# A feed-forward block with seven-product tiles: the token sums are spread over three tiles instead of four

## The chip, the cores and the metric

One Trainium2 chip, one core. The metric is the device time of one execution in microseconds; the median of several runs counts. One execution was profiled.

## The reference

One step of a small hybrid decoder: 512 prompt tokens and 64 sample tokens (8 sequences of 8), width 1024, two layers, all in float32. Each layer has two half-weighted SwiGLU feed-forward blocks around a mixer:

```python
def swiglu(x, wi, wo):
    gate, up = jnp.split(x @ wi, 2, axis=-1)
    return (jax.nn.silu(gate) * up) @ wo
...
h = h + 0.5 * swiglu(rms_norm(h, w['norm_w'][i, 0]), w['ffn1_wi'][i], w['ffn1_wo'][i])
# ... mixer: RWKV-7 in layer 0, dilated window attention in layer 1
h = h + 0.5 * swiglu(rms_norm(h, w['norm_w'][i, 2]), w['ffn2_wi'][i], w['ffn2_wo'][i])
```

The hidden width is 2816. The attention adds a bias that comes from a small table of 32 distance buckets for each head and dilation.

## The kernel before, in words

**Layout.** Activations lie transposed: 128 channels on partitions, 576 tokens along the free axis, in two halves of 288 (h0, h1). The 1024 channels are 8 groups of 128. Each float32 operand is split in a high part (a cast on ScalarE, ACT) and a low part (a subtraction on VectorE, DVE, or on GpSimd, POOL), and a product takes three TensorE passes: high x high, high x low, low x high. Each stretch of weights (128 x 512, 256 KB, tile `wr` or `sr`) is loaded by the queue of SyncE (SP) into one of three buffers, split to `wh`, `wl` (or `sh`, `sl`), and its raw buffer is free for the next load when its last reader is done.

**Two of the four feed-forward blocks are "fast"** (`ffn(..., fast=...)`): the first of layer 0, from 20 us on, and the second of layer 1, from 2450 us on. The hidden width is cut into 22 tiles of 128 columns.

- Tiles 0 to 4 (`pair`) are standard: gate and up, each in two token halves, in four PSUM banks `ps_e`. DVE scales the gate banks by the row norm (L365), ACT applies SiLU, POOL multiplies by the norm again (L368), DVE multiplies the up banks in (L371) and the result is split (L155). Tile 4 goes through its inputs in the outer loop, so it needs all four banks at once.
- Tiles 5 to 21 (`pair7`) take the input and weights as 2 x 2 blocks (channel halves by token halves; weight quarters 11, 21, 22, 12) and make seven block products instead of eight (L390), from sums of weight quarters (`seven`: s1 = 21 + 22, s2 = s1 - 11, s4 = 12 - s2 on DVE at L337, in PSUM; `ss` = 11 - 21 on POOL at L346) and sums of token quarters. Products are issued as 0 to 6 on three banks; bank A is used by products 0, 2, 4 and 6, and is copied or added between them (L396, L402, L407).
- Behind tiles 8, 16 and 21 comes an output part (`wo_part`, L422) on TensorE.

**The token sums** (`forms`) need the normalised input, which the standard tiles do not. For each k of 0 to 3 a step makes from the two channel groups k and k + 4 the products a and b (L292), then c = [a1 - a0, b1 - a1] (halves on DVE L294 and POOL L295) and d = [b1 - c0, b0 - d0] (DVE L296, POOL L297), and splits c and d into `TH`, `TL`. A last step, `quarters`, splits the token quarters a0, b0, b1 into the tiles `x`. The list of these five steps runs one behind each of the tiles 0 to 4 (L437).

**What sets the order.** The program is written tile after tile; a scheduler places each instruction into its engine's queue, and each engine works through its queue in order, waiting on semaphores. So a DVE instruction that waits holds up all behind it.

**The bias tables** are made in the first feed-forward block behind the mixer of layer 0 (1150 to 1240 us): a one-hot matrix `oh` (33 x 1160) is loaded and multiplied by the bias in three pieces (L1288), three times.

## Time and profile before

| | us |
|---|---|
| median of 3 runs (2924.57 to 2925.61) | 2925.57 |
| the profiled execution | 2930.93 |
| its span | 2928.8 |
| TensorE (PE) busy | 2786.2 (95%) |
| DVE busy | 1386.5 (47%) |
| ACT busy | 1198.0 (41%) |
| POOL busy | 1454.0 (50%) |
| mean granted TensorE clock | 0.975 of full speed |

TensorE is busy nearly all the time; the question for any change is which of its few waits it moves. Busy times of the other engines are averages over stages with different limits: in the first 120 us of a fast block DVE, ACT and POOL have the token sums to make beside the weights.

### The profile page before, as it was taken

Reading aid. Unit: us, or ns where it says so; the run is one execution under the profiler, and the core shown is the slowest. Engines: PE = TensorE matmul, PEld = TensorE weight load, DVE = VectorE, ACT = ScalarE, POOL = GpSimd, SP = SyncE. Lnnn points to the kernel's source line nnn. Section 1 sums busy time; section 2 is a strip of 40 time slices with the busy share of each in tenths; the row PEclk is TensorE's granted clock in tenths of the full one; section 3 lists DMA queues with packets and bytes.
Section 4 is the critical chain, followed back from the end, with each engine's and each line's share of the span. In section 5 each row is a group of like instructions: output and inputs, shape, how many; then the busy total and the mean of one; then the engine's idle time right before and its main releaser. Section 6 shows DMA issues by size and latency. Waiting matters only on the chain.

```text
span 2928.8 us, 56127 instructions
## 1 busy us (share of the span) xinstructions
PE 2786.2 (95%) x22360; PEld 2604.7 (89%) x22360; DVE 1386.5 (47%) x2940; ACT 1198.0 (41%) x2296; POOL 1454.0 (50%) x1196
## 2 busy tenths in 40 slices
PE   7899988988999999999999999999999999899997
PEld 7899987977776778999999999999888879899997
DVE  5533338467667654211226321122577775524345
ACT  4434345443333224222335422233456655435354
POOL 6756557553323335444544454454544326757553
PEclk9999998999989899999999999999999999999999
DMA  3233233222113112222233322223433443233223
GB/s 120 81 91 91 87 111 127 70 57 64 44 43 79 40 50 73 85 82 85 83 91 103 96 82 84 83 86 108 131 84 98 132 147 105 80 88 94 87 78 103
DMA packets 177082, 257.81 MB, mean 88 GB/s; under 512 B 46889, under 2 KB 68849, under 8 KB 176820
## 3 DMA queue, kind: packets, MB, share of 16 engines
q1 hardware_dynamic: 148736, 223.56, 25.4%
q10 hardware_dynamic: 28084, 30.66, 3.8%
q8 instruction: 176, 2.88, 0.4%
q14 instruction: 86, 0.70, 0.1%
HBM read 234.31 MB, written 19.85 MB: 87 GB/s over the span
## 4 chain that ended last, share of the span: by engine, by line
PE 71%; DVE 9%; issue 3%; ACT 2%; POOL 2%; DMA 1%; ACTq 0%; DVEq 0%; SPq 0%; POOLq 0%
PE ps_e L196 39%; PE ps_d L517 10%; PE ps_e L390 6%; PE ps_i L517 2%; PE ps_q L517 2%; PE ps_s L517 2%; PE ps_w L517 2%; PE ps_x L517 1%; PE ps_o L517 1%; PE ps_d L390 1%; DVE AR L583 1%; PE ps_pt L526 1%; DVE S L1307 1%; PE ps_d L196 1%; PE ps_y L517 1%
## 5 line engine op out<-in xcount | busy, mean ns | idle before, releaser
L170 POOL TENSOR_TENSOR wl<-wr,wh 128x512 fp32r<-128x512 f32 (+2 forms) x613 | 777.2, 1272 | 975.8 <-ACT wh L169 926.7
L196 PE MATMUL ps_e<-x,wh 128*128 128x288 f32 x3968 | 797.3, 296 | 13.0 <-ACT x L261 7.9
L169 ACT CAST wh<-wr 128x512 fp32r<-128x512 f32 (+2 forms) x613 | 362.2, 594 | 931.7 <-PE ps_e L196 723.8
L196 PEld LDWEIGHTS ps_e<-x,wh 128*128 128x128 f32 x3968 | 639.6, 189 | 18.7 <-ACT x L261 7.9
L196 PE MATMUL ps_e<-hv,wh 128*128 128x288 f32 x2944 | 587.8, 295 | 3.2 <-POOL hv L155 1.9
L196 PE MATMUL ps_e<-x,wl 128*128 128x288 f32 x1984 | 586.5, 296 | 1.4 <-POOL wl L170 1.4
L196 PEld LDWEIGHTS ps_e<-hv,wh 128*128 128x128 f32 x2944 | 472.6, 188 | 4.1 <-POOL hv L155 2.4
L196 PE MATMUL ps_e<-hv,wl 128*128 128x288 f32 x1472 | 434.2, 295 | 1.2 <-POOL wl L170 1.2
L517 PE MATMUL ps_d<-x,wh 128*128 128x288 f32 x1664 | 370.9, 310 | 7.0 <-DVE q L1370 3.3
L196 PEld LDWEIGHTS ps_e<-x,wl 128*128 128x128 f32 x1984 | 373.8, 189 | 2.0 <-POOL wl L170 1.9
L517 PEld LDWEIGHTS ps_d<-x,wh 128*128 128x128 f32 x1664 | 276.1, 192 | 27.5 <-issue 9.3
L196 PEld LDWEIGHTS ps_e<-hv,wl 128*128 128x128 f32 x1472 | 276.8, 188 | 1.5 <-POOL wl L170 1.4
L517 PE MATMUL ps_d<-x,wl 128*128 128x288 f32 x832 | 251.2, 302 | 0.1
L422 DVE SCALAR_TENSOR_TENSOR h<-ps_e,h 128x288 f32<-128x288 f32 x160 | 73.0, 456 | 366.1 <-PE ps_e L196 365.9
L371 DVE TENSOR_TENSOR u<-ps_e,t 128x288 f32<-128x288 f32 x108 | 48.3, 457 | 251.2 <-POOL t L368 142.9
L517 PEld LDWEIGHTS ps_d<-x,wl 128*128 128x128 f32 x832 | 159.9, 192 | 2.2 <-issue 0.5
L365 DVE TENSOR_TENSOR t<-ps_e,rs 128x288 f32<-128x288 f32 x108 | 48.9, 456 | 177.5 <-PE ps_e L196 177.5
L390 PE MATMUL ps_e<-TH,wh 128*128 128x288 f32 x408 | 120.9, 296 | 4.1 <-DVE ev L407 4.0
L390 PE MATMUL ps_e<-TH,wl 128*128 128x288 f32 x408 | 120.3, 295 | 0.0
L390 PE MATMUL ps_e<-TL,wh 128*128 128x288 f32 x408 | 120.2, 295 | 0.0
L1378 POOL TENSOR_TENSOR QS<-q,QS 64x512 fp32r<-64x512 f32 x48 | 63.4, 1321 | 69.2 <-ACT QS L1376 66.6
L332 POOL TENSOR_TENSOR wl<-wr,wh 128x512 fp32r<-128x512 f32 x68 | 88.9, 1310 | 8.7 <-ACT wh L331 5.6
(394 smaller groups left out, 5168.0 us busy)
## 6 DMA issues: line engine op xcount, KB each, us to landing
wr<-in_f1wi SPq DMA_DIRECT2D x142, 256.0 KB
wr<-in_f2wi SPq DMA_DIRECT2D x142, 256.0 KB
wr<-in_f1wo SPq DMA_DIRECT2D x72, 256.0 KB
wr<-in_f2wo SPq DMA_DIRECT2D x72, 256.0 KB
wr<-in_wrkv SPq DMA_DIRECT2D x48, 256.0 KB
wr<-in_wq SPq DMA_DIRECT2D x48, 256.0 KB
sr<-in_f1wi SPq DMA_DIRECT2D x34, 256.0 KB
sr<-in_f2wi SPq DMA_DIRECT2D x34, 256.0 KB
```

The costliest lines, as they stand in the source:

```text
L169: nc.scalar.copy(H, raw)
L170: nc.gpsimd.tensor_tensor(L, raw, H.bitcast(F32), op=ALU.subtract)
L196: nc.tensor.matmul(ps[0:nw], a, b[:, sl], start=k + m == 0, stop=3 * k + m == n - 1)
L332: eng.tensor_tensor(L, a, H.bitcast(F32), op=ALU.subtract)
L365: nc.vector.tensor_tensor(t1[:, sl], ps, rs[:, sl], op=ALU.mult)
L371: nc.vector.tensor_tensor(u[:, sl], ps, t1[:, sl], op=ALU.mult)
L390: nc.tensor.matmul(ps, a, b, start=first and k + m == 0, stop=k == DT // 2 - 1 and m == 2, skip_group_check=True)
L422: nc.vector.scalar_tensor_tensor(h[:, sl], ps, 0.5, h[:, sl], op0=ALU.mult, op1=ALU.add)
L517: self.nc.tensor.matmul(out, lhsT, rhs, **kw)
L526: self.nc.tensor.transpose(out, in_, ident)
L583: nc.vector.scalar_tensor_tensor(m, self.xx[k], self.vec(name, k), self.xn[k], op0=ALU.mult, op1=ALU.add)
L1378: nc.gpsimd.tensor_tensor(qp[H2[1 - par], par], q[o, 0:TP], qp[o, par].bitcast(F32), op=ALU.subtract)
```

## The change

The five steps are spread by a table: step 0 behind tile 0, step 1 behind tile 1, steps 2 and 3 behind tile 2, none behind tile 3, and `quarters` behind tile 4. The last of the four sums, b0 - d0, is written in place over the token half a1, which is not needed any more, and split later by `quarters` together with the quarter a0, as one tile of 576 columns, by DVE for even k and by POOL for odd k. So `TH`, `TL` hold three sums, d is half as wide, and product 6 reads the tile `x`. Around it buffers are made smaller: one `ss` instead of two, five `ev` instead of six, the one-hot matrix in four pieces through one small buffer, the reversed table in two pieces, a smaller scratch for dynamic DMA.

```diff
+STEPS = ((0,), (1,), (2, 3), (), (4,))
...
-            c, d = self.s("t1", self.n_t1), self.s("u", 2)
+            c, d = self.s("t1", self.n_t1), self.s("u", 2)[:, h0]
...
-            nc.vector.tensor_tensor(d[:, h0], b[:, h1], c[:, h0], op=sub)
-            nc.gpsimd.tensor_tensor(d[:, h1], b[:, h0], d[:, h0], op=sub)
...
+            nc.vector.tensor_tensor(d, b[:, h1], c[:, h0], op=sub)
+            nc.gpsimd.tensor_tensor(a[:, h1], b[:, h0], d, op=sub)
+            H, L = (self.ph.tile([128, 3, HF], F32R, name=f"T{x}{k}", tag=f"T{x}{k}") for x in "HL")
+            self.split(c.rearrange("p (z t) -> p z t", z=2), H[:, 0:2], L[:, 0:2], nc.gpsimd)
+            self.split(d, H[:, 2], L[:, 2])
...
-            for k in range(DT // 2):
-                H, L = self.xt(k)
-                self.split(xn[k][0][:, h0], H[:, h0], L[:, h0])
-                out[k].append((H[:, h0], L[:, h0]))
...
+            for z in range(2):
+                for k in range(DT // 2):
+                    H, L = self.xt(k + z * DT // 2)
+                    self.split(xn[k][z], H, L, (nc.vector, nc.gpsimd)[k % 2])
...
-        s3 = self.ph.tile([128, n], F32, name="ss", tag="ss", bufs=2)
+        s3 = self.ph.tile([128, n], F32, name="ss", tag="ss", bufs=1)
...
-                return self.ph.tile([128, HF], F32, name="ev", tag="ev", bufs=6)
+                return self.ph.tile([128, HF], F32, name="ev", tag="ev", bufs=5)
...
-                    if fast:
-                        steps[j]()
+                    for i in STEPS[j] if fast else ():
+                        steps[i]()
...
-        for c in range(0, TBW, 387):
-            e = min(c + 387, TBW)
+        for c in range(0, TBW, 290):
+            e = min(c + 290, TBW)
+            oh = self.sm("oh", [33, 290])
+            nc.scalar.dma_start(oh[:, 0:e - c], self.I["onehot"][g][:, c:e])
...
-    nc = bacc.Bacc("TRN2", target_bir_lowering=False, num_devices=1)
+    nc = bacc.Bacc("TRN2", target_bir_lowering=False, num_devices=1, dynamic_dma_scratch_size=1024)
```

What it does to the queues shows at three places. Lines of the changed kernel are shifted by one to three. First DVE in the first fast block, from the products of step 2 to the split of tile 3's hidden row (the `hv` from `h` are products a and b; `t_595`, `t_747`, `t_611` are c of steps 2, 3 and, in the changed kernel, 3; `t_607` and `t_623` are tile 3's gate). Before:

```order
L292 SCALAR_TENSOR_TENSOR hv<-h_104,vecs,rs 128x576
L292 SCALAR_TENSOR_TENSOR hv<-h_146,vecs,rs 128x576
L294 TENSOR_TENSOR t_595<-hv 128x288
L365 TENSOR_TENSOR t_607<-ps_e,rs 128x288
L296 TENSOR_TENSOR u<-hv,t_595 128x288
L155 TENSOR_TENSOR TL_602<-u,TH_601 128x576
L365 TENSOR_TENSOR t_607<-ps_e,rs 128x288
L371 TENSOR_TENSOR u<-ps_e,t_607 128x288 x2
L155 TENSOR_TENSOR hv<-u,hv 128x576
```

and in the changed kernel:

```order
L294 SCALAR_TENSOR_TENSOR hv<-h_104,vecs,rs 128x576
L294 SCALAR_TENSOR_TENSOR hv<-h_146,vecs,rs 128x576
L296 TENSOR_TENSOR t_595<-hv 128x288
L294 SCALAR_TENSOR_TENSOR hv<-h_104,vecs,rs 128x576
L298 TENSOR_TENSOR u<-hv,t_595 128x288
L294 SCALAR_TENSOR_TENSOR hv<-h_146,vecs,rs 128x576
L296 TENSOR_TENSOR t_611<-hv 128x288
L157 TENSOR_TENSOR TL_602<-u,TH_601 128x288
L298 TENSOR_TENSOR u<-hv,t_611 128x288
L364 TENSOR_TENSOR t_623<-ps_e,rs 128x288 x2
L157 TENSOR_TENSOR TL_618<-u,TH_617 128x288
L370 TENSOR_TENSOR u<-ps_e,t_623 128x288 x2
```

Both scalings of tile 3's gate now stand behind the sums of steps 2 and 3.

Second the start of tile 5. On DVE, from s1 of tile 5 to the scaling of tile 4's gate (`t_759`); `ps_q<-sr,wr` is an s1, `ps_q<-ps_q,wr` an s2, `x` a split token quarter, before:

```order
L337 TENSOR_TENSOR ps_q<-sr,wr 128x512
L155 TENSOR_TENSOR x_901<-hv,x_901 128x288
L155 TENSOR_TENSOR TL_754<-u,TH_753 128x576
L155 TENSOR_TENSOR x_904<-hv,x_904 128x288
L332 TENSOR_TENSOR sl<-ps_q,sh 128x512
L337 TENSOR_TENSOR ps_q<-ps_q,wr 128x512
L155 TENSOR_TENSOR x_907<-hv,x_907 128x576
L332 TENSOR_TENSOR wl<-ps_q,wh 128x512
L337 TENSOR_TENSOR ps_q<-sr,ps_q 128x512
L337 TENSOR_TENSOR ps_q<-sr,wr 128x512
L365 TENSOR_TENSOR t_759<-ps_e,rs 128x288 x2
```

and in the changed kernel:

```order
L336 TENSOR_TENSOR ps_q<-sr,wr 128x512
L157 TENSOR_TENSOR x_895<-hv,x_895 128x576
L331 TENSOR_TENSOR sl<-ps_q,sh 128x512
L336 TENSOR_TENSOR ps_q<-ps_q,wr 128x512
L157 TENSOR_TENSOR x_901<-hv,x_901 128x576
L331 TENSOR_TENSOR wl<-ps_q,wh 128x512
L336 TENSOR_TENSOR ps_q<-sr,ps_q 128x512
L157 TENSOR_TENSOR x_907<-hv,x_907 128x576
L331 TENSOR_TENSOR sl<-ps_q,sh 128x512
L336 TENSOR_TENSOR ps_q<-sr,wr 128x512
L331 TENSOR_TENSOR sl<-ps_q,sh 128x512
L364 TENSOR_TENSOR t_759<-ps_e,rs 128x288 x2
```

The split of the last sum is gone from here, s2 of tile 5 comes earlier in the row, and one more `sl` stands between s1 of tile 6 and the gate scaling.

On POOL at the same place, from the SiLU product of tile 3 (L368) to that of tile 4 (`t_759`), before:

```order
L368 TENSOR_TENSOR t_607<-t_607,rs 128x576
L346 TENSOR_TENSOR ss<-wr,sr 128x512
L170 TENSOR_TENSOR wl<-wr,wh 128x512 x2
L295 TENSOR_TENSOR t_747<-hv 128x288
L346 TENSOR_TENSOR ss<-wr,sr 128x512
L155 TENSOR_TENSOR TL_754<-t_747,TH_753 128x576
L297 TENSOR_TENSOR u<-hv,u 128x288
L332 TENSOR_TENSOR wl<-wr,wh 128x512
L332 TENSOR_TENSOR sl<-sr,sh 128x512
L155 TENSOR_TENSOR x_910<-hv,x_910 128x576
L332 TENSOR_TENSOR wl<-ss,wh 128x512
L368 TENSOR_TENSOR t_759<-t_759,rs 128x576
```

and in the changed kernel:

```order
L367 TENSOR_TENSOR t_623<-t_623,rs 128x576
L345 TENSOR_TENSOR ss<-wr,sr 128x512
L172 TENSOR_TENSOR wl<-wr,wh 128x512 x2
L331 TENSOR_TENSOR sl<-sr,sh 128x512
L157 TENSOR_TENSOR x_898<-hv,x_898 128x576
L331 TENSOR_TENSOR wl<-wr,wh 128x512
L157 TENSOR_TENSOR x_904<-hv,x_904 128x576
L157 TENSOR_TENSOR x_910<-hv,x_910 128x576
L331 TENSOR_TENSOR wl<-ss,wh 128x512
L345 TENSOR_TENSOR ss<-wr,sr 128x512
L331 TENSOR_TENSOR wl<-wr,wh 128x512
L367 TENSOR_TENSOR t_759<-t_759,rs 128x576
```

Two token splits come to POOL, the low half of quarter 11 (`wl<-wr,wh` behind them) stands behind one of them, and the next `ss` stands behind `wl<-ss`. That last shift holds for every tile from 5 on.

Third POOL where the tiles resume behind the first output part (tile 8), before:

```order
L332 TENSOR_TENSOR wl<-ss,wh 128x512
L332 TENSOR_TENSOR wl<-wr,wh 128x512 x2
L346 TENSOR_TENSOR ss<-wr,sr 128x512
L332 TENSOR_TENSOR sl<-sr,sh 128x512
L332 TENSOR_TENSOR wl<-ss,wh 128x512
```

and in the changed kernel:

```order
L331 TENSOR_TENSOR wl<-ss,wh 128x512
L345 TENSOR_TENSOR ss<-wr,sr 128x512
L331 TENSOR_TENSOR wl<-wr,wh 128x512 x2
L331 TENSOR_TENSOR sl<-sr,sh 128x512
L331 TENSOR_TENSOR wl<-ss,wh 128x512
```

The `ss` has moved ahead of the two subtractions, each of which frees a weight buffer. SP's queue is the same in both kernels.

## Rows read from the trace of the kernel before

**Rows 1.** Waits of the whole run: engine, line, waited for; us, times, longest.

```profile
PE ps_e L390 <- DVE t L365: 16.9, 2, 8.5
PE ps_e L390 <- DVE ev L407: 4.0, 4, 1.5
```

**Rows 2.** Timeline of TensorE: start, us, what, [idle before <- releaser].

```profile
94.00 0.82 PE L390 MATMUL ps_e<-x,wh 128*128 128x288 f32 x2 [8.37 <-DVE t L365]
...
97.02 0.39 PE L390 MATMUL ps_e<-TH,sh 128*128 128x288 f32 x1
...
101.85 0.30 PE L390 MATMUL ps_e<-TH,wh 128*128 128x288 f32 x1
...
105.79 0.40 PE L390 MATMUL ps_e<-TH,wh 128*128 128x288 f32 x1 [0.58 <-DVE ev L407]
...
2521.43 0.82 PE L390 MATMUL ps_e<-x,wh 128*128 128x288 f32 x2 [8.54 <-DVE t L365]
...
2533.78 0.29 PE L390 MATMUL ps_e<-TH,wh 128*128 128x288 f32 x1
```

**Rows 3.** Windows: length, busy of PE, PEld, DVE, ACT, POOL; clock, DMA share, GB/s.

```profile
70.00:75.00 5.00, 3.33 (x26) 3.13 (x25) 2.03 (x5) 2.92 (x5) 3.63 (x3) 1.00 0.35 105
...
90.00:95.00 5.00, 1.00 (x4) 1.03 (x5) 4.07 (x7) 4.07 (x8) 2.68 (x2) 0.54 0.38 115
```

**Rows 4.** Timeline of DVE from step 2 to the start of tile 5.

```profile
62.80 1.54 DVE L292 SCALAR_TENSOR_TENSOR hv<-h,vecs,rs 128x576 f32<-128x576 f32 x2
...
70.13 0.44 DVE L365 TENSOR_TENSOR t<-ps_e,rs 128x288 f32<-128x288 f32 x1
72.81 0.82 DVE L371 TENSOR_TENSOR u<-ps_e,t 128x288 f32<-128x288 f32 x2 [2.23 <-POOL t L368]
...
75.95 3.62 DVE L292 SCALAR_TENSOR_TENSOR hv<-h,vecs,rs 128x576 f32<-128x576 f32 x2
...
81.58 0.69 DVE L337 TENSOR_TENSOR ps_q<-sr,wr 128x512 f32<-128x512 f32 x1
...
89.23 0.68 DVE L337 TENSOR_TENSOR ps_q<-ps_q,wr 128x512 f32<-128x512 f32 x1
...
92.79 0.70 DVE L337 TENSOR_TENSOR ps_q<-sr,wr 128x512 f32<-128x512 f32 x1 [0.88 <-DMA wr<-in_f1wi]
93.40 0.81 DVE L365 TENSOR_TENSOR t<-ps_e,rs 128x288 f32<-128x288 f32 x2
```

**Rows 5.** Timeline of POOL, the same stretch.

```profile
64.41 0.96 POOL L295 TENSOR_TENSOR t<-hv 128x288 f32<-128x288 f32 x1 [2.15 <-DVE hv L292]
66.15 1.43 POOL L155 TENSOR_TENSOR TL<-t,TH 128x576 fp32r<-128x576 f32 x1 [0.78 <-ACT TH L154]
67.54 0.80 POOL L297 TENSOR_TENSOR u<-hv,u 128x288 f32<-128x288 f32 x1
68.30 3.06 POOL L170 TENSOR_TENSOR wl<-wr,wh 128x512 fp32r<-128x512 f32 x2
71.37 1.40 POOL L368 TENSOR_TENSOR t<-t,rs 128x576 f32<-128x576 f32 x1
74.12 1.29 POOL L346 TENSOR_TENSOR ss<-wr,sr 128x512 f32<-128x512 f32 x1 [1.35 <-DMA wr<-in_f1wi]
75.38 3.57 POOL L170 TENSOR_TENSOR wl<-wr,wh 128x512 fp32r<-128x512 f32 x2
```

**Rows 6.** Timeline of SP's queue: the load of quarter 22 of tile 6.

```profile
89.98 0.33 SPq L325 DMA_DIRECT2D wr<-in_f1wi  x1
```

**Rows 7.** Timelines of POOL and TensorE where tiles resume behind the second output part.

```profile
334.27 2.54 POOL L332 TENSOR_TENSOR wl<-wr,wh 128x512 fp32r<-128x512 f32 x2
...
342.42 0.40 PE L390 MATMUL ps_e<-TH,wh 128*128 128x288 f32 x1 [0.86 <-DVE ev L407]
```

**Rows 8.** Costliest groups of the page: the weight casts; busy, mean ns | idle before.

```profile
L169 ACT CAST wh<-wr 128x512 fp32r<-128x512 f32 (+2 forms) x613 | 362.2, 594 | 931.7 <-PE ps_e L196 723.8
```

More of the change, by code (lines that the diff above doesn't have):

```diff
@@ L51 @@
 F_STD = 5
+STEPS = ((0,), (1,), (2, 3), (), (4,))
+N_S7 = 4
 F_PARTS = (0, 8, 16, FT)
@@ L292, in sums @@
                 nc.vector.scalar_tensor_tensor(t, self.h[i], self.vec(gain, i), self.rs, op0=ALU.mult, op1=ALU.mult)
-            c, d = self.s("t1", self.n_t1), self.s("u", 2)
+            c, d = self.s("t1", self.n_t1), self.s("u", 2)[:, h0]
             nc.vector.tensor_tensor(c[:, h0], a[:, h1], a[:, h0], op=sub)
             nc.gpsimd.tensor_tensor(c[:, h1], b[:, h1], a[:, h1], op=sub)
-            nc.vector.tensor_tensor(d[:, h0], b[:, h1], c[:, h0], op=sub)
-            nc.gpsimd.tensor_tensor(d[:, h1], b[:, h0], d[:, h0], op=sub)
-            H, L = (self.ph.tile([128, 4, HF], F32R, name=f"T{x}{k}", tag=f"T{x}{k}") for x in "HL")
-            for i, t in enumerate((c, d)):
-                self.split(t.rearrange("p (z t) -> p z t", z=2), H[:, 2 * i:2 * i + 2], L[:, 2 * i:2 * i + 2], (nc.gpsimd, nc.vector)[i])
-            out[k] += [(H[:, i], L[:, i]) for i in range(4)]
+            nc.vector.tensor_tensor(d, b[:, h1], c[:, h0], op=sub)
[3 more added lines that the diff above has]
+            self.split(d, H[:, 2], L[:, 2])
+            out[k] += [(H[:, i], L[:, i]) for i in range(3)]
             xn.append((a, b))
         def quarters():
-            for k in range(DT // 2):
-                H, L = self.xt(k)
-                self.split(xn[k][0][:, h0], H[:, h0], L[:, h0])
-                out[k].append((H[:, h0], L[:, h0]))
-            for k in range(DT // 2):
-                H, L = self.xt(k + DT // 2)
-                self.split(xn[k][1], H, L, (nc.vector, nc.gpsimd)[k % 2])
-                out[k] += [(H[:, h0], L[:, h0]), (H[:, h1], L[:, h1])]
+            for z in range(2):
+                for k in range(DT // 2):
+                    H, L = self.xt(k + z * DT // 2)
+                    self.split(xn[k][z], H, L, (nc.vector, nc.gpsimd)[k % 2])
+                    out[k] += [(H[:, h1], L[:, h1]), (H[:, h0], L[:, h0])] if not z else [(H[:, h0], L[:, h0]), (H[:, h1], L[:, h1])]
         return [lambda k=k: sums(k) for k in range(DT // 2)] + [quarters], out
@@ L328, in form @@
         def form(i, a, eng):
-            pool, x, b = (self.ph, "s", 4) if i % 2 else (self.wp, "w", N_W)
+            pool, x, b = (self.ph, "s", N_S7) if i % 2 else (self.wp, "w", N_W)
             H, L = (pool.tile([128, n], F32R, name=x + y, tag=x + y, bufs=b) for y in "hl")
@@ L1281, in bias_table @@
         nc = self.nc
-        oh = self.sm("oh", [33, TBW])
-        nc.scalar.dma_start(oh, self.I["onehot"][g])
         tb = self.sm("tb", [16, TBW])
-        for c in range(0, TBW, 387):
-            e = min(c + 387, TBW)
+        for c in range(0, TBW, 290):
+            e = min(c + 290, TBW)
+            oh = self.sm("oh", [33, 290])
+            nc.scalar.dma_start(oh[:, 0:e - c], self.I["onehot"][g][:, c:e])
             ps = self.bank("q", e - c)
-            nc.tensor.matmul(ps[0:16], self.rb[:, g * 16:(g + 1) * 16], oh[:, c:e], start=True, stop=True)
+            nc.tensor.matmul(ps[0:16], self.rb[:, g * 16:(g + 1) * 16], oh[:, 0:e - c], start=True, stop=True)
             nc.vector.tensor_copy(tb[:, c:e], ps[0:16])
         nc.scalar.dma_start(self.tab[g * 16:(g + 1) * 16], tb)
-        tr = self.sm("tr", [16, SKW])
-        nc.vector.tensor_copy(tr, tb[:, TBW - 1 - SKW:TBW - 1][:, ::-1])
-        nc.scalar.dma_start(self.rev[g * 16:(g + 1) * 16], tr)
+        n = SKW // 2
+        for c in (0, n):
+            tr = self.sm("tr", [16, n])
+            nc.vector.tensor_copy(tr, tb[:, TBW - 1 - c - n:TBW - 1 - c][:, ::-1])
+            nc.scalar.dma_start(self.rev[g * 16:(g + 1) * 16, c:c + n], tr)
     def softmax(self, S, parts, n, adds):
```

## Prediction

> **What bounds the kernel now.** I read four views, from coarse to fine. The waits of TensorE over the whole run come first [rows 1]: its largest single cause is a wait before L390 for the DVE instruction at L365, 16.9 us in two waits. They are the same place in the two fast feed-forward blocks: the passage from the last standard tile (tile 4) to the first seven-product tile (tile 5). TensorE's timeline shows it [rows 2]: 8.37 us idle before 94.00, so tile 4 had ended at 85.63, and 8.54 us before 2521.43. Outside this the two blocks are bound by TensorE. The clock is the third view [rows 3]: after the idle time the granted clock of 90 to 95 us is 0.54, that is 1.2 GHz for a stretch, while it stayed 1.00 over the shorter wait at 70 to 75. TensorE needs 3.02 us for the 12 matmuls of product 0 (94.00 to 97.02) and 4.83 us for the next 36, 0.252 against 0.134 each, so the slow stretch costs 12 x 0.118 = 1.4 us here. From the first matmul of tile 5 to its product 6 it is 11.79 us in the first block and 12.35 in the second; 72 matmuls at 0.134 are 9.6, so 2.2 and 2.7 us are lost to clock and waits.
>
> Who is late at 94.00? The four PSUM banks of tile 4 must be read before product 0 can write. DVE reads the first at 93.40 [rows 4], though TensorE was done at 85.63. Ahead of it on DVE stands s1 of tile 6 (L337, 92.79), which waits for a weight quarter whose load was issued at 89.98 [rows 6], 2.81 us earlier. The load waited for the buffer of quarter 11 of tile 5, last read by s2 (L337, 89.23), and s2 stood behind the last token sum's splits. So **the wait ends with a buffer and a DMA, not with the arithmetic of the sums**. That is what I follow through the changed order.
>
> **Step 1: two sums behind tile 2.** DVE has two more products, two more half-size subtractions, and TL2 now half-size, ahead of both gate scalings of tile 3; before, one scaling went between and the other followed at 70.13. Two products alone take 1.54 us (62.80), two beside POOL's weight subtractions 3.62 (75.95), and those two POOL instructions 3.57 [rows 4, 5]: the two engines' SBUF-to-SBUF work adds up rather than overlaps. From 64.34 (62.80 + 1.54): DVE 1.54 + 5 x 0.41 = 3.6, and POOL's four instructions in between 0.96 + 1.43 + 0.80 + 1.53 = 4.7. With nothing overlapped the sums end at 72.6, with all overlapped at 67.9; I take 72.5, since the 3.62 row is the nearest. The scalings end at 73.3 instead of 70.6, 2.7 later. POOL then does the fourth sum 0.80, TL3 1.43, a weight subtraction 1.5 and the SiLU product (L368, 1.40) before DVE can free the up banks: up to 77.6 against 72.77, 4.8 later. Between 2.7 and 4.8 I take 3.8. Tile 4 begins 3.8 us later and ends at 89.4. This costs nothing by itself, because step 2 lets tile 5 begin only after 95.
>
> **Step 2: the start of tile 5.** Cover: none, TensorE is idle. POOL's second weight subtraction of tile 4 ended at 71.36 and `ss`, which needs the load that this frees, began at 74.12, 2.76 later [rows 5]. Now it ends at about 75.2, `ss` runs 78.0 to 79.3, the third subtraction ends at 80.6, and the quarter 22 of tile 5 that takes its buffer lands 2.8 later, at 83.4. So s1 of tile 5 is at 83.4, not 81.58 [rows 4]. From there the gain of the change shows: the split of the last sum and three split halves no longer stand ahead of s2. But the buffer of quarter 11 is now held by POOL. After s1 (0.6) and two casts of 0.6 (ACT, [rows 8]) POOL runs `sl` 1.3, the split of token quarter x1, which moved to it, 1.4, and only then the low half of 11, 1.3; with 0.7 for DVE's x2 between, it is free at 89.9, against 89.98 before. **The new wait takes the place of the old one.** The load lands at 92.7, then s1 of tile 6 (0.6). The order also puts one more `sl` (0.6), which waits for the cast of that s1 (0.6), ahead of the gate scaling: 94.6 instead of 93.40, **1.2 us later**. Ends: 0.6 us earlier if s1 of tile 5 is not late, 2.2 later if every POOL instruction meets DVE's.
>
> **Step 3: inside tile 5.** TensorE's product 4 writes bank A again, which ACT must have copied. ACT does that behind the cast of tile 4's hidden row, that behind DVE's u, that behind POOL's SiLU product, and POOL now does `wl` of form 4, the next `ss` and another `wl` first. From 93.3: three casts 1.8, POOL 1.3 + 1.3 + 1.3 + 1.4 and 0.4 of port wait, DVE 0.8, ACT 0.6 + 0.4 + 1.1 + 0.4: product 4 at 104.1 instead of 101.85, 2.3 late; product 6 waits for DVE's L407 behind s1 of tile 7, up to 0.9 more. I take product 6 **2.8 us late** in the first block, at 108.6, which is 13.4 after product 0. A slow clock of up to 2.7 us is inside these waits. The second block, with the same 13.4, comes out at 1.2 + 13.4 - 12.35 = **2.2 late**. Steps 1 to 3: 5.0 us.
>
> **Step 4: one `ss` buffer.** `ss` of the next tile now follows `wl` of the present one on POOL and holds up the next subtractions. In the steady run of seven-product tiles TensorE hides it. Four times, where tiles resume behind an output part, it stands ahead of the two subtractions that free the next weight buffers (334.27, 2.54 us), and TensorE already waits there for L407 behind s1 and its DMA, 0.86 us at 342.42 [rows 7]; [rows 1] has four such waits in all, one of them the 0.58 at 105.79. Each is at most one `ss`, 1.29, and at least 0. I take 0.9, nearer the top because 342.42 shows no slack: 4 x 0.9 = **3.6 us** (0 to 5.2).
>
> **The rest.** The bias table loads its one-hot rows in four pieces through one buffer: nine times a load must land while 18 other matmuls run, 18 x 0.134 = 2.4 us. A 256 KB load took 2.81; a piece is a seventh of that. Between 0 and 9 x 0.7 = 6 us I take **0.4**, near zero. ACT casts the same columns as before. POOL gets two token splits more (2.8 us a block), DVE less; both are counted in step 2. Product 6 reads x instead of TH, the same 12 matmuls. `ev` with 5 buffers: a tile takes 4. The smaller scratch for dynamic DMA: every DMA here is on hardware or instruction queues, 0.
>
> **The sum:** 5.0 + 3.6 + 0.4 = 9.0 us. Against the profiled execution, 2930.93 us, that is 2939.9, 0.31% more; on the median of the runs, 2925.57, it is **2934.6**.
>
> **Rivals.** *The wait shrinks* (the other side). If quarter 11's buffer goes with s2 and not with POOL's low half, the load is issued at about 87.1, DVE reads tile 4's banks at about 91.6 and tile 5 starts at 92.2: 1.8 earlier, TensorE is idle for 3 us only and stays at 2.4 GHz, 1.4 and 2.7 back. 2 x 1.8 + 4.1 = 7.7 us less, 2917.9, with steps 3 and 4 at zero. It decides itself at POOL: its three instructions (4.0 us) must end by s2's end. For it: DVE's own queue does get shorter. Against: POOL was already the slower engine of the two (two subtractions 3.57). 0.10.
>
> *Nothing to see.* Step 3's waits lie within the slow clock that the first matmuls have anyway, and step 4 finds slack: 2 x 1.2 + 0.4 = 2.8, 2928.4. For it: 2.2 and 2.7 us are already lost behind product 0. 0.22.
>
> *The clock falls twice.* TensorE's wait before tile 4 grows from under 2 us to over 5. The granted clock stayed at 1.00 over the short wait and fell behind the long one [rows 3], so tile 4 may begin at 1.2 GHz and end 1.4 to 2.7 later. It then gives up its first weight buffers later, and the cast of quarter 11 needs one: about 1.3 us of this reaches tile 5, 2 x 1.3 = 2.6 more, 2937.2, at worst the whole 2 x 2.7, 2940. 0.12. "TensorE: Matmul & The Clock Gate" of the Trainium skill (Part 1) has the array throttled by default and released by activity; by that rule alone the clock would fall and the time be 2937.2; the trace bears it out for 8.4 us of idle time and not for 1.7, and shows none of 5 us in this place.
>
> The other rule that bears on step 1 is in "SBUF — State Buffer" of the Trainium skill (Who interferes with whom): a VectorE instruction with two SBUF inputs and a GpSimd instruction that reads SBUF exclude each other for the whole instruction. By it step 1's sum is the 72.6 of the unoverlapped end, by full overlap it would be 67.9, with tile 4 barely later.
>
> **How the numbers follow.** My forecast, 2934.6, has 0.56; its own range, from the ends of steps 2 to 4, is 2929 to 2940. A change of under 0.2%, 5.9 us, cannot be told from none here: faster is under 2919.7, slower over 2931.4. Slower: 0.48 of the forecast and all of the clock's 0.12, 0.60. Same: 0.08 and 0.22, 0.30. Faster: 0.10. The range of 8 in 10 goes from 2925 to 2940: it leaves out the 0.10 of the faster rival and some 0.08 above and below.
>
> **What would show it.** Step 1: the wait before tile 4 (L196 for DVE L371) grows from 1.7 us (5.00 less 3.33 in [rows 3]) to about 5.5. Step 2: the wait before product 0 of tile 5 falls from 8.4 to about 6, yet that product begins 1 to 2 us later after tile 2 than before, with a load issued right behind POOL's low half. Step 3: new TensorE waits at L390 inside tile 5, on ACT and POOL, of 1 to 2 us each. Step 4: the four waits for L407 about 1 us longer each. I am wrong if the wait before product 0 falls under 4 us in both blocks, or if the waits for L407 stay as they are.

## The result and the profile after

The changed kernel took **2943.95 us** (median of four executions, 2939.84 to 2946.81) against 2925.07 for the kernel before: a ratio of 1.0066, 95% interval 1.0049 to 1.0084, so 14 to 25 us slower. On another occasion six executions gave 2938.29 against 2924.22, ratio 1.0052 (1.0034 to 1.0070), 10 to 21 us. The forecast was 2934.6, +9.0 us, with a range up to 2940: the sign and the place were right, and the size was about half to two thirds of what was measured. The first median lies above the range, the second inside it. One execution of the kernel before (10579.25 us) and one of e7 below (4373.15 us) lie far outside all others and are in no ratio.

In the changed kernel's code the lines of the rows shown before have shifted: L390 is L389, L365 is L364, L371 is L370, L407 is L406, L337 is L336. The waits of TensorE over the whole run (us in total, times, longest) answer to [rows 1]:

```profile
PE ps_e L389 <- DVE t L364: 9.7, 2, 5.0
PE ps_e L198 <- DVE u L370: 8.4, 2, 4.2
PE ps_e L389 <- DVE ev L406: 8.3, 6, 3.3
```

The 16.9 us before product 0 have become 9.7, but 8.4 us stand before tile 4, where 3.6 stood, and the waits for the eviction at L406 have doubled, from 4.0 to 8.3. TensorE's timeline answers to [rows 2]; in brackets is the idle time before and what ended it:

```profile
76.93 0.82 PE L198 MATMUL ps_e<-x,wh 128*128 128x288 f32 x2 [4.20 <-DVE u L370]
...
95.52 0.82 PE L389 MATMUL ps_e<-x,wh 128*128 128x288 f32 x2 [5.04 <-DVE t L364]
...
108.15 0.54 PE L389 MATMUL ps_e<-x,wh 128*128 128x288 f32 x2 [0.36 <-DVE ev L406]
...
2524.90 0.82 PE L389 MATMUL ps_e<-x,wh 128*128 128x288 f32 x2 [4.64 <-DVE t L364]
...
2537.66 0.54 PE L389 MATMUL ps_e<-x,wh 128*128 128x288 f32 x2 [0.39 <-DVE ev L406]
```

Product 0 begins 1.5 us later than in [rows 2] and product 6 2.4 later. These are times from the start of the span, and the blocks do not begin at the same time in both profiles: the first begins 1.1 us earlier in the changed kernel (26.55 against 27.63, the rows of L276 and L274 below) and the second 2.2 later. From the start of its block product 6 is 3.4 us later in the first and 1.7 in the second. The windows of the same stretch answer to [rows 3] (length, busy time of PE, PEld, DVE, ACT, POOL, then the granted clock, DMA share, GB/s):

```profile
76.00:80.00 4.00, 3.07 (x13) 3.10 (x14) 2.56 (x3) 1.34 (x2) 2.56 (x3) 0.57 0.18 64
...
95.00:100.00 5.00, 4.48 (x19) 4.51 (x20) 2.96 (x5) 2.96 (x6) 4.47 (x4) 0.50 0.06 19
```

So the clock is at 1.2 GHz at the start of tile 4 and again at the start of tile 5. DVE's and SP's timelines answer to [rows 4] and [rows 6]:

```profile
76.33 0.82 DVE L370 TENSOR_TENSOR u<-ps_e,t 128x288 f32<-128x288 f32 x2 [2.51 <-POOL t L367]
...
92.78 0.89 DVE L336 TENSOR_TENSOR ps_q<-sr,wr 128x512 f32<-128x512 f32 x1 [1.68 <-DMA wr<-in_f1wi]
94.32 0.69 DVE L331 TENSOR_TENSOR sl<-ps_q,sh 128x512 fp32r<-128x512 f32 x1 [0.65 <-ACT sh L330]
94.93 0.81 DVE L364 TENSOR_TENSOR t<-ps_e,rs 128x288 f32<-128x288 f32 x2
```

```profile
89.91 0.33 SPq L324 DMA_DIRECT2D wr<-in_f1wi  x1
```

The load goes out as POOL ends the low half of quarter 11 (89.88), and not at the end of s2, which DVE had done by 86.15:

```profile
88.59 1.29 POOL L331 TENSOR_TENSOR wl<-wr,wh 128x512 fp32r<-128x512 f32 x1
```

To set the two fast blocks apart from the rest I measure each from the matmul of the ones ahead of it to its last residual update. For the kernel before (TensorE, then DVE):

```profile
27.63 1.24 PE L274 MATMUL ps_q<-ssum,ones 128*128 128x288 f32 x4 [3.57 <-DVE ssum L268]
...
2450.42 1.24 PE L274 MATMUL ps_d<-S,ones 128*128 128x288 f32 x4 [1.11 <-DVE S L268]
```

```profile
428.22 0.46 DVE L422 SCALAR_TENSOR_TENSOR h<-ps_e,h 128x288 f32<-128x288 f32 x1 [0.91 <-PE ps_e L196]
...
2858.52 0.45 DVE L422 SCALAR_TENSOR_TENSOR h<-ps_e,h 128x288 f32<-128x288 f32 x1
```

That is 400.59 and 408.10, **808.7 us** for both. For the changed kernel:

```profile
26.55 2.29 PE L276 MATMUL ps_q<-ssum,ones 128*128 128x288 f32 x4 [3.56 <-DVE ssum L270]
...
2452.64 1.24 PE L276 MATMUL ps_d<-S,ones 128*128 128x288 f32 x4 [1.08 <-DVE S L270]
```

```profile
434.01 0.46 DVE L421 SCALAR_TENSOR_TENSOR h<-ps_e,h 128x288 f32<-128x288 f32 x1 [0.91 <-PE ps_e L198]
...
2867.38 0.45 DVE L421 SCALAR_TENSOR_TENSOR h<-ps_e,h 128x288 f32<-128x288 f32 x1
```

407.46 and 414.74, **822.2 us**: 13.5 more. Yet the two spans differ by 9.3 only (2938.1 against 2928.8). The difference lies in a stretch that the change does not touch, the mixer of layer 0. Its window in the profile of before, and then in that of after:

```profile
800.00:1100.00 300.00, 289.15 (x3055) 210.59 (x3053) 204.20 (x582) 97.99 (x235) 99.69 (x98) 0.93 0.19 53
```

```profile
800.00:1100.00 300.00, 288.97 (x3117) 209.45 (x3115) 211.96 (x593) 102.27 (x249) 108.60 (x105) 0.96 0.19 53
```

The profiled execution of before did 62 matmuls fewer in these 300 us at a lower granted clock; at the window's mean of 0.098 us each that is about 6 us. The whole stretch between the two fast blocks says the same: 2022.2 us before and 2018.6 after, though the latter has 2 us more for the bias table (e4 and e6 below). Among the fourteen profiles of this study only one other, that of e7 below, falls under 0.94 there, with 0.92. It was an execution with bad luck in a place of no interest, 5 us over its own median, and it hid about 6 of the 15.6 us that the change costs in the fast blocks and the bias table. That the forecast made against it (2939.9) meets the profiled time of after (2939.84) is therefore chance.

### The profile page after: what moved, and what is told of

It reads as the page before. It is cut to its first block, busy times and chain, and to the rows that moved or that the text cites. A ratio compares the mean times of both kernels' runs of the same rounds, so it can differ in the third digit from the quotient of the medians.

```text
span 2938.1 us, 56209 instructions
## 1 busy us (share of the span) xinstructions
PE 2791.7 (95%) x22366; PEld 2607.2 (89%) x22366; DVE 1391.2 (47%) x2942; ACT 1196.8 (41%) x2296; POOL 1458.2 (50%) x1200
## 4 chain that ended last, share of the span: by engine, by line
PE 79%; DVE 9%; issue 4%; POOL 3%; ACT 2%; DMA 2%; DVEq 0%; SPq 0%; ACTq 0%; POOLq 0%
PE ps_e L198 43%; PE ps_d L516 11%; PE ps_e L389 10%; PE ps_i L516 2%; PE ps_s L516 2%; PE ps_q L516 2%; PE ps_w L516 2%; PE ps_d L389 2%; PE ps_x L516 1%; PE ps_o L516 1%; PE ps_pt L525 1%; DVE S L1308 1%; POOL wl L172 1%; PE ps_d L198 1%; PE ps_i L525 1%
## 5 line engine op out<-in xcount | busy, mean ns | idle before, releaser
L198 PE MATMUL ps_e<-x,wh 128*128 128x288 f32 x3968 | 801.2, 297 | 18.1 <-DVE u L370 8.4
L198 PEld LDWEIGHTS ps_e<-x,wh 128*128 128x128 f32 x3968 | 641.9, 189 | 26.1 <-issue 14.6
L370 DVE TENSOR_TENSOR u<-ps_e,t 128x288 f32<-128x288 f32 x108 | 48.4, 457 | 259.0 <-POOL t L367 152.4
L389 PE MATMUL ps_e<-x,wh 128*128 128x288 f32 x544 | 115.7, 307 | 18.0 <-DVE t L364 9.7
L364 DVE TENSOR_TENSOR t<-ps_e,rs 128x288 f32<-128x288 f32 x108 | 48.8, 456 | 171.1 <-PE ps_e L198 171.1
L389 PEld LDWEIGHTS ps_e<-x,wh 128*128 128x128 f32 x544 | 91.1, 197 | 20.2 <-ACT wh L330 10.1
L1308 DVE TENSOR_TENSOR S<-S 128x256 f32<-128x256 f32 (+4 forms) x160 | 86.8, 560 | 10.6 <-ACT S L150 10.5
```

The costliest lines, as they stand in the source:

```text
L198: nc.tensor.matmul(ps[0:nw], a, b[:, sl], start=k + m == 0, stop=3 * k + m == n - 1)
L364: nc.vector.tensor_tensor(t1[:, sl], ps, rs[:, sl], op=ALU.mult)
L370: nc.vector.tensor_tensor(u[:, sl], ps, t1[:, sl], op=ALU.mult)
L389: nc.tensor.matmul(ps, a, b, start=first and k + m == 0, stop=k == DT // 2 - 1 and m == 2, skip_group_check=True)
L1308: nc.vector.tensor_tensor(S[:, a], S[:, a], S[:, b], op=ALU.add)
```

## The experiments

Each experiment was timed against the kernel before on the same chip, with 12 executions unless said otherwise. There were three occasions, each on its own chip: e1 to e4, e5 to e8, e9 to e12; across them compare the ratios. The interval of a ratio is about 0.15% to either side, 4 us, so I read each twice: by the median, and in its profile by the length of the two fast blocks, measured as above.

| kernel | median us | ratio to before (95%) | fast blocks us, against 808.7 |
|---|---|---|---|
| before | 2924 to 2926 | 1 | 808.7 |
| changed, first | 2943.95 (4) | 1.0066 (1.0049 to 1.0084) | 822.2, +13.5 |
| e1 changed, again | 2938.29 (6) | 1.0052 (1.0034 to 1.0070) | 819.9, +11.2 |
| e2 order back | 2932.97 | 1.0034 (1.0018 to 1.0050) | 815.6, +6.9 |
| e3 two s3 buffers | 2932.11 | 1.0030 (1.0017 to 1.0044) | 813.8, +5.1 |
| e4 bias table whole | 2929.42 | 1.0020 (1.0005 to 1.0036) | 813.7, +5.0 |
| e5 before, one s3 buffer | 2928.11 | 1.0011 (0.9997 to 1.0025) | 815.4, +6.7 |
| e6 before, bias pieces | 2924.24 | 1.0002 (0.9988 to 1.0016) | 809.9, +1.2 |
| e7 order and sums alone | 2934.05 | 1.0028 (1.0015 to 1.0040) | 813.8, +5.1 |
| e9 sums alone | 2923.50 | 0.9991 (0.9979 to 1.0003) | 809.0, +0.3 |
| e8 order, fourth raw buffer | 2918.89 | 0.9980 (0.9967 to 0.9993) | 805.4, -3.3 |
| e11 changed, fourth raw buffer | 2918.73 | 0.9979 (0.9967 to 0.9992) | 804.1, -4.6 |
| e10 order back, fourth raw buffer | 2914.66 (10) | 0.9965 (0.9951 to 0.9979) | 803.4, -5.3 |
| e12 the same, fourth sr buffer | 2915.68 | 0.9965 (0.9951 to 0.9979) | 802.5, -6.2 |

### e1: the changed kernel again

> The changed kernel once more, unaltered. Its four executions so far lay 19 us over the kernel before at the median, but its profiled one only 9 us over the profiled one of before, which is what my steps account for. Theory 1 (the gap is real and of every execution, the profiled ones are lucky or unlucky by some us): about 2944 us again, 18 us over the kernel before, and again 2938 to 2947 between executions. Rival (the gap is a matter of that chip and hour): 2934 to 2938, some 9 us over the kernel before on the same chip. The profiled execution should again show 9.7 us of waits before L389 for the gate scaling at L364, 8.4 before tile 4 at L198 and 8 us at L406.

2938.29 us, 14.1 over the kernel before: between the two, and the intervals of both occasions share 14 to 20 us. Its profile repeats the waits of after (8.7, 8.5 and 8.4 us for the three causes). So the gap is real, and larger than the 9 us between the two profiled executions.

### e2: one step behind each tile again

```diff
-STEPS = ((0,), (1,), (2, 3), (), (4,))
+STEPS = ((0,), (1,), (2,), (3,), (4,))
```

> The changed kernel with one step behind each of the first five tiles again (as before); the four three-part sums, the single buffer of s3, the bias table in pieces and the smaller buffers stay. Theory 1 (my steps 1 to 3: the order costs 5 us, mostly at the start of the first seven-product tile, and one buffer of s3 costs 3.6): 5 us under the changed kernel on the same chip. Rival A (the order costs all 19, since the clock falls at two places in each block and what follows is late too): 15 to 19 us under it, level with the kernel before within 0.2%. Rival B (order costs nothing, all lies in the single buffer of s3 or the bias pieces): within 2 us of the changed kernel.

5.3 us less than the changed kernel by the median, 4.3 to 6.6 by the fast blocks (against e1 and against the first profile): theory 1. The waits move back where they were:

```profile
PE ps_e L389 <- DVE t L364: 16.0, 2, 8.0
PE ps_e L389 <- DVE ev L406: 8.8, 7, 3.3
PE ps_e L198 <- DVE u L370: 2.1, 2, 1.2
```

The 8.8 us at L406 stay: they are not the order's.

### e3 and e5: the single buffer of s3

e3 gives the changed kernel its second buffer back, e5 takes it from the kernel before.

```diff
-        s3 = self.ph.tile([128, n], F32, name="ss", tag="ss", bufs=1)
+        s3 = self.ph.tile([128, n], F32, name="ss", tag="ss", bufs=2)
```

> The changed kernel with two buffers for s3 in place of one, nothing else. Theory 1 (my step 4: four places where the seven-product tiles resume, 0.9 us each): 3.6 us under the changed kernel, and the waits at L406 for ev fall from 8.3 us to about 4. Rival A (the single buffer costs what my sum lacks, since every load that it holds up is late by a time that changes from execution to execution): 10 to 13 us under the changed kernel, and executions closer together. Rival B (it costs nothing, the waits at L406 have another cause): within 1 us, waits at L406 still 8 us.

> The kernel before with one buffer for s3 in place of two, nothing else. Theory 2, from the profiles after the first experiments (the single buffer makes the seven-product tiles late where they resume after a block of output tiles, and the clock falls in the wait; the four places together cost 7 to 9 us in the profiles with one buffer, and about 0 in the one with two): 6 to 9 us over the kernel before, waits at L407 for ev about 8 us in place of 4. Theory 1 (my step 4): 3.6 us over it. Rival (the cost comes only together with the new order, which already keeps the loads late): within 2 us of the kernel before, waits at L407 of 4 to 5 us.

e3 came out 6.2 us under the changed kernel, between my 3.6 and rival A. e5 came out 4.3 over the kernel before, with an interval of -1 to +7 that holds no change, my 3.6 and the low end of theory 2's 6 to 9; it decides little alone. The fast blocks say 6.1 to 8.4 for e3 and 6.7 for e5. The waits of e3 and of e5 for the eviction:

```profile
PE ps_e L389 <- DVE ev L406: 3.6, 5, 1.1
```

```profile
PE ps_e L390 <- DVE ev L407: 8.8, 6, 3.3
```

With one buffer they are 8.3 to 8.8 us in four profiles, with two 3.6 to 5.4 in five others. The exception is e4, below. The place is not the same in every kernel: in e5 3.85 of the 8.8 us stand before product 6 of tile 5 (1.93 at 105.58 and 1.92 at 2525.29, against 0.58 and none in the kernel before), with a clock of 0.66 behind each, while the wait before product 0 falls from 16.9 to 13.6; in the changed kernel 7.6 of the 8.3 stand where tiles resume. How one buffer does it is seen in the changed kernel where tiles resume behind the first output part, POOL first:

```profile
194.41 1.30 POOL L331 TENSOR_TENSOR wl<-ss,wh 128x512 fp32r<-128x512 f32 x1 [4.76 <-ACT wh L330]
195.79 1.30 POOL L345 TENSOR_TENSOR ss<-wr,sr 128x512 f32<-128x512 f32 x1
197.04 2.54 POOL L331 TENSOR_TENSOR wl<-wr,wh 128x512 fp32r<-128x512 f32 x2
```

SP's queue, DVE and TensorE behind it:

```profile
197.11 0.33 SPq L324 DMA_DIRECT2D sr<-in_f1wi  x1
...
199.61 0.33 SPq L324 DMA_DIRECT2D wr<-in_f1wi  x1
```

```profile
203.09 1.62 DVE L336 TENSOR_TENSOR ps_q<-sr,wr 128x512 f32<-128x512 f32 x1 [1.83 <-issue]
...
205.23 0.44 DVE L406 TENSOR_TENSOR ev<-ps_e,ev 128x288 f32<-128x288 f32 x1
```

```profile
205.72 0.53 PE L389 MATMUL ps_e<-x,wh 128*128 128x288 f32 x2 [1.93 <-DVE ev L406]
```

The next s3 must wait until the last one has been subtracted (194.41), and stands ahead of the two subtractions that give two raw buffers back (197.04 to 199.58). The load at 199.61 goes out as the second ends. DVE's s1 begins 3.48 us later; the view names no releaser for its wait (`issue`), and that it waits for this load is read from the times. The eviction at L406 stands behind s1, and TensorE waits for that. In the kernel before the next s3 was made at 184.52 already, s1 took 0.70 us in place of 1.62, and TensorE has no wait here:

```profile
184.52 1.29 POOL L346 TENSOR_TENSOR ss<-wr,sr 128x512 f32<-128x512 f32 x1 [2.98 <-DMA wr<-in_f1wi]
```

```profile
199.74 0.70 DVE L337 TENSOR_TENSOR ps_q<-sr,wr 128x512 f32<-128x512 f32 x1 [0.88 <-DVE t L404]
```

Behind the wait of the changed kernel the clock falls too:

```profile
200.00:205.00 5.00, 3.79 (x29) 3.56 (x27) 3.17 (x5) 1.41 (x3) 2.88 (x3) 1.00 0.47 141
205.00:210.00 5.00, 4.28 (x20) 4.28 (x21) 2.69 (x6) 2.37 (x4) 2.47 (x3) 0.66 0.16 52
```

In its 4.28 busy microseconds TensorE began 20 matmuls, where 0.134 each would make 32: 12 fewer, so 1.6 us more beside the 1.93 of the wait. But the same wait at the second block's second resumption, in the same profile, has nothing behind it:

```profile
2780.30 0.54 PE L389 MATMUL ps_e<-x,wh 128*128 128x288 f32 x2 [1.93 <-DVE ev L406]
```

```profile
2780.00:2785.00 5.00, 4.70 (x35) 4.70 (x36) 2.27 (x5) 2.90 (x5) 3.40 (x4) 1.00 0.18 52
```

So a wait of this length costs its own time, and in some places the slow clock besides.

### e4 and e6: the bias table

e4 is the changed kernel with the old function of the bias table, e6 the kernel before with the new one. The core of the edit, as in e6:

```diff
-        oh = self.sm("oh", [33, TBW])
-        nc.scalar.dma_start(oh, self.I["onehot"][g])
-        for c in range(0, TBW, 387):
+        for c in range(0, TBW, 290):
+            oh = self.sm("oh", [33, 290])
+            nc.scalar.dma_start(oh[:, 0:e - c], self.I["onehot"][g][:, c:e])
```

> The changed kernel with the bias table as before: the one-hot rows loaded whole (one load for each group), pieces of 387 columns, and the reversed row in one piece. Theory 1 (the bias table costs 0.4 us): within 1 us of the changed kernel. Rival (its smaller and more numerous loads delay others in the same queue, or move where the table is made, by an amount that differs from execution to execution): 5 to 10 us under the changed kernel.

> The kernel before with the bias table in pieces of 290 columns with their own loads, nothing else. Theory 2 (the pieces stand one by one between matmuls of the feed-forward tiles and cost 2.1 us in every profile that has them, between 1160 and 1270 us): 2 us over the kernel before, and 1160 to 1260 holds about 15 matmuls fewer than before. Theory 1 (my 0.4 us): within 0.5. Rival (they cost most of the 9 us by which the kernel with the whole table was shorter at the median): 5 to 9 us over it.

By the medians the two disagree: e4 lies 8.9 us under the changed kernel, which is what the rival said, e6 only 0.5 over the kernel before (-3.5 to +4.7), which rules its rival out. The profiles settle what the table itself costs. In its stretch the kernel before and the changed kernel show, in this order:

```profile
1145.00:1275.00 130.00, 130.00 (x944) 123.84 (x943) 35.23 (x60) 35.79 (x57) 63.14 (x48) 1.00 0.28 84
```

```profile
1145.00:1275.00 130.00, 129.93 (x934) 122.00 (x933) 38.95 (x65) 35.83 (x57) 63.04 (x48) 1.00 0.28 82
```

944 matmuls of which 18 are the table's, against 934 with 24: 16 ordinary ones fewer, at 0.134 that is **2.1 us**. From the block's first read of the up banks (DVE, L371 or L370) to its last residual update all eight profiles with the whole table take 415.0 us and all six with pieces 416.9 to 417.1, which is the same 2 us. About half of it is plain work: 18 matmuls took 486 ns each, 24 pieces 409, 8.75 against 9.82 us in all; the other half I did not take apart. The rest of e4's gain lies in the fast blocks, whose code that edit does not touch: 813.7 us, where the same code had 822.2 and 819.9. In the first block its waits for L406 are those of the changed kernel; it has the 1.93 too (before 205.14), but the clock stays at 1.00 behind it (205 to 210, 36 matmuls in place of 20). Its waits at L406 were 4.3 us in all in place of 8.3 and 8.5, and the difference is in the second block. There the two part at a load. In the changed kernel it went out at 2611.98 and s1 could use it 3.83 us later; in e4 it was 2.66. SP and DVE of the changed kernel, then of e4:

```profile
2611.98 0.33 SPq L324 DMA_DIRECT2D wr<-in_f2wi  x1
```

```profile
2615.81 0.70 DVE L336 TENSOR_TENSOR ps_q<-sr,wr 128x512 f32<-128x512 f32 x1 [4.28 <-DMA wr<-in_f2wi]
...
2634.47 1.05 DVE L336 TENSOR_TENSOR ps_q<-sr,wr 128x512 f32<-128x512 f32 x1 [3.74 <-DMA wr<-in_f2wi]
```

```profile
2606.60 0.33 SPq L324 DMA_DIRECT2D wr<-in_f2wi  x1
```

```profile
2609.26 0.70 DVE L336 TENSOR_TENSOR ps_q<-sr,wr 128x512 f32<-128x512 f32 x1 [3.01 <-DMA wr<-in_f2wi]
...
2626.74 0.70 DVE L336 TENSOR_TENSOR ps_q<-sr,wr 128x512 f32<-128x512 f32 x1 [1.29 <-issue]
```

Two tiles later s1 is 18.66 us behind the first in the changed kernel and 17.48 in e4, and TensorE waits 3.27 us at 2636.53 in the one and 0.47 in the other. e1 and e2 have the late load too (3.74 and 3.71 us) and the same wait of 3.27. But e5, with the sums of before, had its load in 2.72 us and waits 3.26, so that this one load does not settle it in every kernel. What is shown is that with one buffer the resumption has no slack left, and that the same code of the block paid 3.3 us there or 0.5. Why e4 got through stays open. It need not be the luck of one execution: the profiled one (2928.84 us) is typical of e4's twelve, whose median, 2929.42, lies 8.9 us under e1's. Nor is it shown to come from the edit: the intervals of e1 and e4 still touch (from 1.0034, up to 1.0036). Undone one by one, order, s3 buffer and bias table give back 5.3, 6.2 and 8.9 us, 20.4 where there are 14.1 to give back, and it is e4 that does not fit.

### e7 and e9: the order and the sums without the rest

e9 is the kernel before with the three-part sums alone, e7 has the new order as well; buffers, bias table and scratch are those of before.

> The changed kernel with only the new order and the three-part sums: two buffers for s3, the bias table whole, six ev buffers and the scratch of before. Theory 2 (the order costs my steps 1 to 3, 4 to 5 us in both blocks together, and nothing else does): 3 to 6 us over the kernel before, 9 to 11 under the changed kernel's median, waits before tile 4 of 4.2 us as in the changed kernel, the two waits at L389 for the gate scaling 10 us. Rival (the order also makes the resumptions late): 8 us or more over the kernel before, waits at L406 of 6 to 8 us.

> The kernel before with only the three-part sums (forms with three tiles and the quarters split whole): order, two buffers for s3, bias table, six ev buffers and scratch as before. Theory 2 (they cost nothing; the whole loss is the order, the single buffer of s3 and the bias pieces): within 3 us of the kernel before, 6 to 10 under the order alone; the wait before tile 4 at 1 to 2 us, the two waits at L389 for the gate scaling at about 16. Rival (part of what was put down to the order comes from the sums' new form, whose extra cast on ACT and subtraction on POOL stand at the start of tile 5): 4 us or more over the kernel before.

e9 is 2.4 us under the kernel before, with an interval that holds no change; no cost of the sums shows. e7 is 10.3 over by its median, which is the rival's 8 or more, and 4 to 12 by the interval, which holds theory 2's 3 to 6 in part. Its fast blocks are 5.1 longer than those of before and 4.8 longer than those of e9. They equal those of e3 (813.8 both), which has five `ev` buffers and the small scratch, so no cost of these two shows there. The order alone makes the wait before tile 4 and the slow clock behind it (TensorE and a window of e7):

```profile
76.62 0.82 PE L198 MATMUL ps_e<-x,wh 128*128 128x288 f32 x2 [4.21 <-DVE u L370]
```

```profile
75.00:79.00 4.00, 2.38 (x10) 2.41 (x11) 2.24 (x3) 1.24 (x2) 2.63 (x3) 0.54 0.20 66
```

In e9 the same wait is 1.56 us. The rival's mechanism, late resumptions by the order, falls: the waits at L406 are 4.1 us, as in the kernel before. What the median has above the 5 us of the blocks is not placed.

### e8, e10, e11, e12: a fourth raw buffer

If a weight buffer that comes free late sets the start of tile 5, one more must move it. The memory of the fourth sum and of the smaller scratch holds it.

```diff
-                r = self.wp.tile([128, n], F32, name="wr", tag="wr", bufs=N_W - 1)
+                r = self.wp.tile([128, n], F32, name="wr", tag="wr", bufs=N_W)
```

(and the same at the two other places that use this buffer). e8 has the new order, two buffers for s3 and the whole bias table; e10 also has the order of before and six ev buffers; e11 is the changed kernel and this edit alone; e12 is e10 with `tag="sr", bufs=4`.

> The new order and sums with two buffers for s3 and the bias table whole, and the memory that the three-part sums and the small scratch leave goes to a fourth raw weight buffer wr, which the loads of one-sided quarters share. Theory 2 (product 0 of tile 5 is late because a quarter of tile 6 is loaded only when quarter 11 of tile 5 gives its buffer back, and DVE waits for it ahead of tile 4's scalings): with a fourth buffer the load starts earlier, s1 of tile 6 no longer waits, the 5 us wait at L389 for the gate scaling falls to 1 or 2, and the kernel comes out 3 to 10 us under the kernel before. Rival (the next wait, for a cast or a sum on POOL, takes its place): within 3 us of the order alone.

> The fourth raw buffer with one step behind each of the first five tiles again (the rest as in the kernel with the fourth raw buffer). Theory 2 (with the buffer the 16 us wait for the gate scaling goes, and without the new order the 4 us waits before tile 4 and the fall of the clock there go too): 3 to 6 us under the new order with the fourth buffer, 8 to 11 under the kernel before. Rival (the new order is what makes room for the quarters' splitting once the load is early: it must be made between tile 4 and tile 5, and product 0 then waits for it): 0 to 5 us over the new order with the fourth buffer.

> The changed kernel with the fourth raw buffer wr alone: new order, one buffer for s3, bias table in pieces. Theory 2 (the single buffer of s3 makes the resumptions late because it holds the raw quarters that it is made from, and so the next loads; a fourth raw buffer takes that away too): 16 to 20 us under the changed kernel, within 4 us of the same kernel with two s3 buffers and the whole bias table, waits at L406 for ev 1 to 3 us in place of 8.5. Rival (s3 is late by its own buffer, not by the loads): 8 to 12 us under the changed kernel, waits at L406 still 6 to 8 us.

> Order back, fourth raw buffer wr and a fourth raw buffer sr for the other two quarters. Theory 2 (what the loads of wr held up is gone with the fourth wr, and sr is not the last to come free): within 2 us of order back with the fourth wr. Rival (the four raw quarters of a tile come free together, so that the waits at the start of tile 5 and at the resumptions only go with both): 3 us or more under it.

By their times all four came out about where theory 2 has them, and all four beat both kernels. The waits of e11, the changed kernel with one raw buffer more:

```profile
PE ps_e L198 <- DVE u L370: 14.5, 4, 4.2
...
PE ps_e L389 <- DVE ev L406: 1.1, 2, 0.5
```

The waits for the gate scaling at L364 are gone altogether, and those at L406 fall from 8.3 to 1.1 though s3 has its single buffer: with a raw quarter to spare, that buffer does no harm that shows. What is left in e8 and e11 is 14.5 us before and inside tile 4, 4.2 and 3.1 in each block; in e10 this:

```profile
PE ps_e L198 <- DVE u L370: 9.2, 4, 3.4
...
PE ps_e L389 <- DVE t L364: 7.6, 2, 4.0
```

The 4.2 us waits before tile 4 are gone with the old order, but a wait of 3.3 to 3.4 inside tile 4 stays and 7.6 us stand before product 0 again, which theory 2 for e10 had not expected; the sum of these waits is not smaller than in e11. With the fourth raw buffer the old order is 4.1 us shorter than e11 at the medians, on the same chip, and 0.7 in the fast blocks; the two intervals overlap, so that it is better is likely and not shown. **The lowest median is e10's, 2914.66 us, 0.35% under the kernel before (0.21 to 0.49%).** A fourth buffer for the other two quarters adds nothing that can be told (e12).

## Why the prediction was right in sign and short in size

**Steps 1 to 3, 5.0 us: right in the sum.** e7 less the kernel before gives 5.1 us in the fast blocks, e7 less e9 4.8, and the medians of e2 5.3. By product 6, from the start of each block, the changed kernel lost 3.4 and 1.7 us where 2.8 and 2.2 were forecast, so the two errors cancel. Part of the agreement below is luck: the forecast times count from the kernel before, and step 2's products began at 62.30 and not at 62.80, so that what follows took half a microsecond longer than forecast.

- Step 1. The up banks of tile 3 were read at 76.33; 72.81 in [rows 4] plus the 3.8 taken is 76.6. The gate scalings ended at 71.9 and not at 73.3, so DVE overlapped more than I let it; POOL's product (74.90 to 76.29) still came last, and it decides. DVE's sums made way for the scalings at 71.11, nearer to the unoverlapped end of 72.6 than to the overlapped 67.9. The rule of the Trainium skill's "SBUF — State Buffer" (Who interferes with whom), which excludes the two engines from each other, agrees with this for the most part.
- Step 2. s1 of tile 5 was put at 83.4 and began at 83.50; the load of quarter 22 at 89.9, issued at 89.91; s1 of tile 6 at 92.7, began at 92.78; the gate scaling at 94.6, began at 94.93. The wait of 8.4 us fell to 5.0 without a gain, as the text said: the buffer came free when it had before, with POOL's low half (89.88). e8 and e11 show that this buffer was the cause.
- Step 3. Product 6 began at 108.15, forecast 108.6. The way there was another: no waits for ACT or POOL show inside tile 5, which I had named as the sign of this step (e1 has one, of 0.70 us). From product 0 to product 6 it took 12.63 and 12.76 us, not 13.4. TensorE did its first 20 matmuls at half pace (0.50 in the window of 95 to 100), and under that the casts and evictions came in time. The slow clock took the place of the waits. What this step had too much went to product 0: counted from the start of its block it was 2.6 us later in the first block and 1.3 in the second, where step 2 has 1.2.

**Step 4, 3.6 us: mis-sized; this is the step that failed.** The mechanism was as described (s3 ahead of the two subtractions that free the buffers), but it cost 6.7 us in e5, and 6.1 to 8.4 between the changed kernel and e3. I priced each place at 0.9 because one wait of 0.86 stood in [rows 7], and held one `ss`, 1.29, for the most that a place can cost. The resumptions of the changed kernel show waits of 1.93, 0.47, 3.27 and 1.93. At the first, s1 began 3.48 us behind its load's issue and took 1.62 us itself, so more than one `ss` stood ahead of the eviction, and behind the wait a clock of 0.66 cost 1.6 us more. I had the slow clock behind the waits of tile 5 in the sum, and not behind these. Nor are all four waits of [rows 1] at a resumption: the 0.58 at 105.79 is inside tile 5, and in e5 3.85 of the 8.8 us of these waits stand there.

**The bias table, 0.4 us: mis-sized.** 2.0 us in its own block in every profile that has the pieces. I counted the loads, found them hidden, and did not count that 24 matmuls of 290 columns take 1.07 us more than 18 of 387; that alone is half of it. Whether the pieces cost more than this together with the single s3 buffer, as e4's 8.9 us would have it, stays open.

**The sum.** 5.0 + 6.7 + 2.1 = 13.8 us by the profiles, with e3's 6.1 to 8.4 in place of e5's 6.7 it is 13.2 to 15.5, against 14.1 measured on the second occasion and 18.9 on the first, whose interval begins at 14.3. The remaining 5 us of the first occasion I cannot put to a place: executions of one kernel lie 20 us and more apart, and the four of that day have one profile. My range ended at 2940 since it took step 4's upper end, 5.2, from waits without their clock.

**The rivals.** *The wait shrinks* did not happen: it needed POOL to be done by s2's end, 86.15, and POOL was done at 89.88. *Nothing to see* was wrong: steps 1 to 3 alone cost more than its 2.8 us. *The clock falls twice* came true in its first half: a wait of 4.20 us before tile 4, 0.57 behind it, tile 4 ending at 90.48 (95.52 less 5.04) and not at 89.4. But this did not reach tile 5, since product 0 waited for DVE until 95.52 anyway. The 1.00 behind 1.67 us before tile 4 in the kernel before [rows 3], and the 0.66 and the 1.00 behind two waits of 1.93 in the changed kernel, show that the length of the one wait does not tell it alone. The rule of "TensorE: Matmul & The Clock Gate" (Part 1 of that page of the Trainium skill), that the array is throttled by default and activity releases it, agrees with the 0.57 behind 4.20 us and does not by itself tell the two waits of 1.93 apart.

## What to carry to other kernels

When a wait ends with a buffer that is given back and a load behind it, follow the buffer through the change and not the arithmetic: the instruction that last reads it sets the start, and one buffer more was worth about 20 us to the changed kernel, where its new order had cost 5. Price a small wait in a stretch that TensorE bounds with and without the slow clock that may stand behind it: it nearly doubled one wait of 1.93 us here and left another as it was. And before a sum is made against a profiled execution, look in a stretch that the change leaves alone whether that execution is a typical one.
